# Second layer's projection weights: split into high and low parts ahead of time, or when they are used

## The chip, the cores and the metric

The kernel runs on one core of a Trainium2 chip. The metric is the time of one execution on the device, in microseconds (us), as the median of several runs. One execution was also taken with the hardware profiler; all rows below come from it.

## The reference

A stream of 512 latent tokens and a prefix of 256 context tokens, 1024 wide, pass through two layers. Cut to what matters here, a layer does:

```python
hl = modulate(rms_norm(x_lat, norm1_g), sh1, sc1)
p  = hl @ w_in            # columns: A (gMLP), Q, K, V, C (convolution), 512 each
pa, q, k, v, pc = split(p)                        # q, k: norm per head, rotary
ya = chunk_gmlp(pa)       # gelu, layer norm, 128x128 position mixing
o  = diff_attn(q, k_all, v_all)                   # keys: latent and context
yc = silu(layer_norm(dwconv31(glu(pc))))
x  = x + g1 * (concat(ya, rms_norm(o), yc) @ w_out)
h2 = modulate(rms_norm(x, norm2_g), sh2, sc2)
x  = x + g2 * ((silu(dwconv3(h2 @ w_gate)) * (h2 @ w_val)) @ w_down)
```

The first layer does this for latent and context tokens alike. In the second layer the context tokens only give keys and values. All numbers are float32, and the result has to be as close as float32 makes it.

## The kernel before

**Split products.** TensorE multiplies a reduced float32 form (float32r). To keep the precision, each operand is split into a high part, the value cast to float32r, and a low part, the value minus the high part, and a product is three matmuls: high by high, high by low, low by high. For activations this is done once. For a weight chunk it is done where the chunk is used: `wsplit` (L215) loads a raw chunk of 128x1024 on SP's queue (L212, tile `raw`, three buffers), casts it on ScalarE (L220, tile `whi`, two buffers) and subtracts on VectorE or GpSimd (`sub_lo`, L106, tile `wlo`, two buffers). The string `WE` says for each chunk of w_in which of the two engines subtracts (d or p), with one string for each layer.

**The order of the second layer.** A projection (`proj_tok`, L381) takes four chunks of w_in (128x1024 each, two blocks of the contraction), and for each chunk goes through its token tiles. The order is: K for the two context tiles, C (L432), A, K for the four latent tiles, Q, V for all six tiles; then attention in 16 units, with products of w_out as filler, then the rest of w_out and the feed-forward part. K's four chunks are thus split twice. Hooks at fixed steps of a projection put other work between its matmuls: the gate products `pg` of group A (L226 to L228 by the helper, from `vbh` of L496) and the transposes `pk` of K (L577, from `ks`).

**VectorE's work at that time.** The convolution of group C is 60 multiply-adds on VectorE (L647, tile `cacc`), at low priority. Beside them stand the statistics of A's layer norm (L482), its scaling (L494, L495), the norm and rotary of K and Q (L552 to L568, L591) and the low parts. GpSimd makes the rotary tables GC and GS (L543, L544), clears the convolution's input (L420) and has small copies and diagonals in attention.

**The feed-forward part** of the first layer runs in two halves of 11 blocks. In each half, 11 times, a gate and a value block are multiplied, convolved, gated and split into `gh` and `gl`; then four pairs of output blocks go through w_down in three chunks each. The rows of the adaLN modulation are computed on VectorE during the first half (`start_dots`, L918).

**What sets the order.** The program is written in plain order; a planner then orders the instructions of each engine by a priority that follows the program, by which `high_priority` moves instructions ahead and `low` back, and by its own estimate of when operands are ready. On the chip each engine and each queue keeps that order strictly: an instruction that waits holds up all behind it on its engine. Transfers issued on an engine's queue are instructions of that engine. All transfers of the kernel before are issued by SP. The kernel is built with `_BACC = {"dynamic_dma_scratch_size": 256}` (L1092), which the change leaves as it is.

Of the kernel before, what the change touches and what calls it, by code (L numbers as in the profile page):

```python
# [9 lines left out]
F32 = mybir.dt.float32  # L10
F32R = mybir.dt.float32r
# [40 lines left out]
DLOW, RLOW = 150, 250  # L52
CLOW = (4000, 1000)

WE = ("dpdpdpdddppdpppppddp", "pdpppppppppppppddpdd")

AH = ((4, 1), (18, 1))
KH = ((6, 10, 27, 31, 35, 39), (17, 17, 25, 34, 35, 48))
CH = ((41, 3), (40, 5))
N1H, N1P = 5, 2  # L60

VEV = 2

# [13 lines left out]
def tile_backbone(  # L77
# [137 lines left out]
    def wsplit(src, shape, eng="mix", raw=None, p=None, tags=("hi", "lo"), bufs=2):  # L215
# [6 lines left out]
            sub_lo(lo, raw, hi, e)  # L222
        return hi, lo

    def mm3(o, lhi, llo, rhi, rlo, start, stop):
        T.matmul(o, lhi, rhi, start=start, stop=False)  # L226
        T.matmul(o, lhi, rlo, start=False, stop=False)  # L227
        T.matmul(o, llo, rhi, start=False, stop=stop)  # L228
# [53 lines left out]
    for l in range(DEPTH):  # L282
# [26 lines left out]
        with ExitStack() as ph:  # L309
# [2 lines left out]
            ps = psum_pool(ph, f"ps1_{l}")  # L312

            def wengine(col, k2):
                return {"d": "dve", "p": "pool"}[WE[l][(col - COL_A) // 512 * 4 + k2]]

            def wsrc(col, k2):
                return w_in[l, 2 * k2 * P:(2 * k2 + 2) * P, col:col + 512].rearrange("(a p) n -> p a n", p=P)

            if l == 0:  # L320
                cs = sp.tile([P, KD, 32], F32, name="cs")
# [59 lines left out]
            def proj_tok(col, tiles, hooks=(), back=False):  # L381
                hooks, step = list(hooks), 0
                pt = {t: ps.tile([P, 512], F32, tag="acc", name="acc", bufs=6) for t in tiles}
                for k2 in range(KD // 2):
                    wh, wl = wsplit(wsrc(col, k2), [2, 512], wengine(col, k2))
                    for t in tiles:
                        for a in range(2):
                            hs = (slice(None), 2 * k2 + a, slice(t * P, (t + 1) * P))
                            T.matmul(pt[t], hhi[hs], wh[:, a], start=k2 + a == 0, stop=False)  # L389
                            T.matmul(pt[t], hlo[hs], wh[:, a], start=False, stop=False)  # L390
                        step += 1
                        for _, fn in [h for h in hooks if h[0] == step]:
                            fn()
                    for t in list(tiles)[::-1] if back and k2 == 3 else tiles:
                        for a in range(2):
                            hs = (slice(None), 2 * k2 + a, slice(t * P, (t + 1) * P))
                            T.matmul(pt[t], hhi[hs], wl[:, a], start=False, stop=k2 + 1 == KD // 2 and a == 1)  # L397
                        step += 1
                        for _, fn in [h for h in hooks if h[0] == step]:
                            fn()  # L400
                for _, fn in [h for h in hooks if h[0] > step]:
                    fn()
                return pt
# [26 lines left out]
                for o in px:  # L430
                    T.matmul(o.rearrange("p a n -> p (a n)"), z[:, :P], z, start=True, stop=False)
            for k2 in range(KD // 2):  # L432
                wh, wl = wsplit(wsrc(COL_C, k2), [2, 512], wengine(COL_C, k2), raw=pre.get(k2))
                for a in range(2):
                    k = 2 * k2 + a
                    for s in range(nseg)[::-1]:
                        t0, t1 = SEG[s]
                        for m in range(4):
                            ms = slice(m * P, (m + 1) * P)
                            o = pc[s][m][:, :t1 - t0]  # L440
                            T.matmul(o, wh[:, a, ms], hhi[:, k, t0:t1], start=k == 0 and s == 0, stop=False)
                            T.matmul(o, wh[:, a, ms], hlo[:, k, t0:t1], start=False, stop=False)
                            T.matmul(o, wl[:, a, ms], hhi[:, k, t0:t1], start=False,
                                     stop=k == KD - 1 and (s == 0 or m % 2 == 1))
# [50 lines left out]
            V.tensor_add(v, v, lnv[:, 1].unsqueeze(1).to_broadcast([P, NT, AW]))  # L495
            S.copy(vbh, v)  # L496
            sub_lo(vbl, v, vbh)
            wsh, wsl = wsplit(w_sT[l], [HEADS, P], p=sp, **(dict(bufs=1) if l else dict(tags=("mraw", "mraw"), bufs=MRB)))
            def a_finish():
                for h in range(HEADS):  # L500
                    yield
# [38 lines left out]
            nc.sync.dma_start(out=gbase, in_=qk_g[l])  # L540
            V.tensor_scalar_mul(gbase[:, 0], gbase[:, 0], QKD ** -0.5)
            for j in range(2):
                G.tensor_mul(GC[:, j], ropet[:, 0], gbase[:, j, 0].unsqueeze(1).to_broadcast([P, NLT, QKD]))  # L543
                G.tensor_mul(GS[:, j], ropet[:, 1], gbase[:, j, 1].unsqueeze(1).to_broadcast([P, NLT, QKD]))  # L544

            def qk_tile(x, t, j, r):

# [139 lines left out]
        yBl = yp.tile([P, 4, toks], F32R, name="yBl")  # L687

        def wout_w(mp2, parts, eng, **kw):
            return [(wsplit(w_out[l, q, mp2], [2, 4, P], eng, **kw), (yACh, yACl) if q == 0 else (yBh, yBl))  # L690
                    for q in parts]

        def wout(mp2, parts, w, segs, psf, tag, bufs, only=(0, 1)):
# [221 lines left out]
        with ExitStack() as ph:  # L915
# [22 lines left out]
            for half in range(2):  # L938
                gh = hp.tile([P, HJ, toks], F32R, tag="gh", name="gh", bufs=1)
                gl = hp.tile([P, HJ, toks], F32R, tag="gl", name="gl", bufs=1)  # L940
                for jj in range(HJ):
                    j = half * HJ + jj
                    pp = [[ps.tile([P, 512], F32, tag="acc", name="pp", bufs=8) for g in range(2)]
                          for s in range(nseg)]
                    w = [wsplit(w_gv[l, j, g], [KD, P], "dve") for g in range(2)]

                    def gv(g, seg):
                        a, b, s = seg
                        o = pp[s][g][:, a - SEG[s][0]:b - SEG[s][0]]
                        for k in range(KD):  # L950
                            mm3(o, w[g][0][:, k], w[g][1][:, k], hhi[:, k, a:b], hlo[:, k, a:b], k == 0, k == KD - 1)

                    if j == 0:
                        for seg in ngs:
                            if seg == g1:
                                for k in range(KD):
                                    r = norm2.apply(l, 1, g1, k, hhi, hlo)
                                tab["since"].append(r.ins)
                                table(T_SILU)
                            for g in range(2):  # L960
                                gv(g, seg)
                                if seg == g0 and g == 1:
                                    norm2.rstd(g1, ps, "acc", 8)
                    else:
                        for g in range(2):
                            for seg in whole:
                                gv(g, seg)
                    if j == 0 and not last:
                        start_dots(norm2.last)
                    t = sp.tile([P, TOK], F32, tag="ft", name="ft", bufs=FTB)  # L970
                    for s in range(nseg):
                        a, b = SEG[s]
                        gp = pp[s][0]
                        n = b - a
                        S.activation(t[:, a:b], gp[:, :n], AF.Identity, bias=fb[:, l, j:j + 1], scale=fw[:, l, j, 1:2])
                        V.scalar_tensor_tensor(out=t[:, a + 1:b], in0=gp[:, 0:n - 1], scalar=fw[:, l, j, 0:1],
                                               in1=t[:, a + 1:b], op0=ALU.mult, op1=ALU.add)
                        V.scalar_tensor_tensor(out=t[:, a:b - 1], in0=gp[:, 1:n], scalar=fw[:, l, j, 2:3],
                                               in1=t[:, a:b - 1], op0=ALU.mult, op1=ALU.add)
                    act(t[:, :toks], t[:, :toks], AF.Silu)  # L980
                    for s in range(nseg):
                        a, b = SEG[s]
                        V.tensor_mul(t[:, a:b], t[:, a:b], pp[s][1][:, :b - a])  # L983
                    S.copy(gh[:, jj], t[:, :toks])
                    sub_lo(gl[:, jj], t[:, :toks], gh[:, jj])
                chunks = [(j0, min(4, HJ - j0)) for j0 in range(0, HJ, 4)]
                for mp2 in range(KD // 2):
                    tail = half == 1 and mp2 == KD // 2 - 1
                    ws = {}
                    for gi, gs in enumerate([[g] for g in ngs] if tail else [whole]):  # L990
                        pd = {g: [ps.tile([P, 512], F32, tag="acc", name="pd", bufs=8) for i in range(2)] for g in gs}
                        cs_ = chunks[::-1] if gi else chunks
                        for ci, (j0, jn) in enumerate(cs_):
# [4 lines left out]
                            for jj in range(jn):  # L998
                                if gi and not last and (ci, jj) == (0, N1P):
                                    next_norm(ngs[0], ps, "acc", 8)  # L1000
                                st_, sp_ = ci == 0 and jj == 0, ci == len(cs_) - 1 and jj == jn - 1
                                for g in gs:
                                    a, b, s = g
                                    for i in range(2):
                                        ms = slice(i * P, (i + 1) * P)
                                        mm3(pd[g][i][:, :b - a], wh[:, jj, ms], wl[:, jj, ms],
                                            gh[:, j0 + jj, a:b], gl[:, j0 + jj, a:b], st_, sp_)
                        for g in gs:
                            a, b, s = g
                            for i in range(2):  # L1010
# [13 lines left out]
                if not last and half == 0:  # L1024
                    dots.close()
                    cstack.close()
                    wt = pool(ph, "wt", "left")
        pss_.close()
    hbs.close()
    nstack.close()  # L1030
# [84 lines left out]
```

## Time and profile before

| | |
|---|---|
| median of 3 runs | 1636.67 us (1635.95 to 1638.53) |
| the profiled execution | 1637.72 us, of which the span (first to last instruction) 1635.9 us |
| mean granted TensorE clock | 0.986 |
| TensorE (PE) busy | 1574.7 us, 96% |
| VectorE (DVE) busy | 1033.9 us, 63% |
| ScalarE (ACT) busy | 646.2 us, 40% |
| GpSimd (POOL) busy | 178.3 us, 11% |
| DMA | 162.08 MB, mean 99 GB/s |

Busy times of matmuls overlap at their ends, so a busy TensorE is not one at its peak. Rows of the trace name line, engine, operation and tiles as out<-in; a helper's line stands for all its callers, so the tile tells which call it is. A wait is put down to the instruction that released it. The second layer begins at about 968 us of the span, its attention at about 1143 us.

### The profile page before, as it was taken

The page shows a single profiled execution, that of the slowest core. Times are in us where ns is not written, and L with a number is a line of the kernel's source. Part 1 is how long each engine was busy: PE and PEld are TensorE (multiplying, and loading weights), DVE is VectorE, ACT ScalarE, POOL GpSimd, SP SyncE. Part 2 cuts the span into 40 slices and gives each one's busy share as a digit, 9 for nine tenths or more (in the row PEclk, how much of TensorE's full clock was granted, in tenths as well). Part 3 has the DMA queues.
Part 4 walks back from the last instruction along what each step waited for, and adds up shares of the span by engine and source line. Part 5 has one row for each costly group of instructions (what it writes and reads, how often), then busy time and mean ns, then how long its engine had stood idle before and what let it go on. Part 6 is the DMA issues. An engine that isn't in the chain of part 4 may idle for free.

```text
span 1635.9 us, 20796 instructions
## 1 busy us (share of the span) xinstructions
PE 1574.7 (96%) x8186; PEld 1294.7 (79%) x8186; DVE 1033.9 (63%) x1666; ACT 646.2 (40%) x1098; POOL 178.3 (11%) x158
## 2 busy tenths in 40 slices
PE   7999998999999999999999999779999999999999
PEld 5865776778888888888888878567778788888888
DVE  4597878969999862244333277996987544244433
ACT  5431568753523221133232244255775433123321
POOL 1130224310000000000000023341420000000000
PEclk8999999999999999999999999889999999999999
DMA  8625110014355852111122223221001223332232
GB/s 286 201 96 171 42 62 14 14 64 169 104 193 194 290 192 70 66 65 62 56 65 58 84 87 110 62 65 52 27 27 65 91 90 96 88 101 97 96 100 94
DMA packets 57409, 162.08 MB, mean 99 GB/s; under 512 B 9056, under 2 KB 11360, under 8 KB 57184
## 3 DMA queue, kind: packets, MB, share of 16 engines
q1 hardware_dynamic: 57312, 160.76, 30.3%
q8 instruction: 64, 1.05, 0.3%
q14 instruction: 33, 0.27, 0.0%
HBM read 158.64 MB, written 2.10 MB: 98 GB/s over the span
## 4 chain that ended last, share of the span: by engine, by line
PE 83%; DVE 10%; ACT 4%; issue 1%; DMA 1%; POOL 0%; POOLq 0%; DVEq 0%; SPq 0%; ACTq 0%
PE pp L227 13%; PE pp L226 13%; PE pp L228 13%; PE pd L228 6%; PE pd L226 6%; PE pd L227 6%; PE acc L389 4%; PE acc L390 4%; PE acc L397 3%; DVE cacc L647 3%; PE po L816 2%; PE mr L156 2%; PE wo L226 1%; PE wo L227 1%; PE wo L228 1%
## 5 line engine op out<-in xcount | busy, mean ns | idle before, releaser
L220 ACT CAST whi<-raw 128x1024 fp32r<-128x1024 f32 (+2 forms) x199 | 204.3, 1029 | 550.9 <-PE pp L227 251.0
L106 DVE TENSOR_TENSOR wlo<-raw,whi 128x1024 fp32r<-128x1024 f32 (+1 forms) x163 | 196.9, 1210 | 304.9 <-ACT whi L220 297.4
L227 PE MATMUL pp<-hlo,whi 128*128 128x512 f32 (+1 forms) x1072 | 380.7, 356 | 0.8 <-DVE hlo L266 0.8
L226 PE MATMUL pp<-hhi,whi 128*128 128x512 f32 (+1 forms) x1072 | 379.8, 356 | 1.5 <-ACT whi L220 1.3
L228 PE MATMUL pp<-hhi,wlo 128*128 128x512 f32 (+1 forms) x1072 | 378.9, 354 | 0.0
L226 PEld LDWEIGHTS pp<-hhi,whi 128*128 128x128 f32 x1072 | 201.4, 188 | 35.1 <-ACT whi L220 2.7
L227 PEld LDWEIGHTS pp<-hlo,whi 128*128 128x128 f32 x1072 | 201.5, 188 | 33.0 <-DVE hlo L266 1.5
L228 PEld LDWEIGHTS pp<-hhi,wlo 128*128 128x128 f32 x1072 | 201.5, 188 | 31.0
L106 POOL TENSOR_TENSOR wlo<-raw,whi 128x1024 fp32r<-128x1024 f32 (+1 forms) x36 | 100.3, 2788 | 870.3 <-ACT whi L220 716.9
L228 PE MATMUL pd<-gh,wlo 128*128 128x512 f32 (+1 forms) x550 | 192.4, 350 | 0.6 <-DVE wlo L106 0.6
L226 PE MATMUL pd<-gh,whi 128*128 128x512 f32 (+1 forms) x550 | 192.9, 351 | 0.0
L227 PE MATMUL pd<-gl,whi 128*128 128x512 f32 (+1 forms) x550 | 192.3, 350 | 0.0
L389 PE MATMUL acc<-whi,hhi 128*128 128x512 f32 x352 | 144.8, 411 | 2.8 <-ACT whi L220 2.8
L390 PE MATMUL acc<-whi,hlo 128*128 128x512 f32 x352 | 144.2, 410 | 0.0
L647 DVE SCALAR_TENSOR_TENSOR cacc<-cin,cw,cacc 128x783 f32<-128x783 f32 (+1 forms) x120 | 125.8, 1102 | 2.8 <-ACT cacc L642 2.7
L228 PEld LDWEIGHTS pd<-gh,wlo 128*128 128x128 f32 x550 | 103.4, 188 | 15.9 <-DVE wlo L106 0.8
L227 PEld LDWEIGHTS pd<-gl,whi 128*128 128x128 f32 x550 | 103.5, 188 | 15.1
L226 PEld LDWEIGHTS pd<-gh,whi 128*128 128x128 f32 x550 | 103.4, 188 | 14.9
L983 DVE TENSOR_TENSOR ft<-ft,pp 128x256 f32<-128x256 f32 (+1 forms) x66 | 39.4, 598 | 96.2 <-PE pp L228 84.7
L397 PE MATMUL acc<-wlo,hhi 128*128 128x512 f32 x352 | 94.0, 401 | 0.0
L389 PEld LDWEIGHTS acc<-whi,hhi 128*128 128x128 f32 x352 | 68.0, 193 | 25.0 <-issue 7.1
L192 DVE CUSTOM_DVE_ANT_0 mraw<-mraw,csil,bmod 128x1024 f32<-128x1024 f32 x64 | 81.7, 1280 | 8.0 <-DMA mraw<-in_w_modT_dram 7.8
(198 smaller groups left out, 2334.3 us busy)
## 6 DMA issues: line engine op xcount, KB each, us to landing
raw<-in_w_gv_dram SPq DMA_DIRECT2D x88, 512.0 KB, 3.2
mraw<-in_w_modT_dram SPq DMA_DIRECT2D x64, 512.0 KB, 4.2
raw<-in_w_in_dram SPq DMA_DIRECT2D x44, 512.0 KB, 3.6
raw<-in_w_down_dram SPq DMA_DIRECT2D x34, 512.0 KB, 3.6
mraw<-in_w_modN_dram SPq DMA_DIRECT2D x16, 512.0 KB, 5.9
mraw<-in_w_modH_dram SPq DMA_DIRECT2D x16, 512.0 KB, 3.9
raw<-in_w_out_dram SPq DMA_DIRECT2D x16, 512.0 KB, 3.2
raw<-in_w_down_dram SPq DMA_DIRECT2D x16, 384.0 KB, 3.2
```

The lines of the kernel that those rows point to most:

```text
L106: (eng or V).tensor_sub(o, a, hi.bitcast(F32))
L156: T.matmul(o[r:r + 32], cs[:, k], w, start=k < 4, stop=k >= 4, tile_position=(0, r))
L192: r = V.tensor_tensor_reduce(out=junk, in0=w, in1=csil[:, s], scale=1.0, scalar=bmod[:, l, i, f:f + 1], op0=ALU.mult, op1=ALU.add, accum_o ...
L220: S.copy(hi, raw)
L226: T.matmul(o, lhi, rhi, start=start, stop=False)
L227: T.matmul(o, lhi, rlo, start=False, stop=False)
L228: T.matmul(o, llo, rhi, start=False, stop=stop)
L389: T.matmul(pt[t], hhi[hs], wh[:, a], start=k2 + a == 0, stop=False)
L390: T.matmul(pt[t], hlo[hs], wh[:, a], start=False, stop=False)
L397: T.matmul(pt[t], hhi[hs], wl[:, a], start=False, stop=k2 + 1 == KD // 2 and a == 1)
L647: V.scalar_tensor_tensor(out=cacc[:, c, :cn], in0=cin[:, c, j:j + cn], scalar=cw[:, l, c, j:j + 1], in1=cacc[:, c, :cn], op0=ALU.mult, op1 ...
L983: V.tensor_mul(t[:, a:b], t[:, a:b], pp[s][1][:, :b - a])
```

## The change

High and low parts of the second layer's w_in (20 chunks) and w_out (8 chunks) are made during the second half of the first layer's feed-forward part and stored in device memory. `split_ahead` is a generator of 56 units: each loads half a chunk (128x512), casts it on ScalarE, subtracts on VectorE and stores both parts; all three transfers are issued by GpSimd. After each of the 11 gate and value blocks three units are drawn (`AHEAD[0]`), after each chunk of w_down eight (`AHEAD[1]`), until none is left, with a priority 60 places later. In the second layer `wsplit_of` loads the two ready parts of a chunk, again on GpSimd's queue; in w_in every second chunk uses two of the three `raw` buffers for its parts. GC and GS, in both layers, move from GpSimd to VectorE, and the low part of w_s is always made on VectorE. The second string of `WE` goes.

```diff
+AHEAD = (3, 8)
+ALOW = 60
+    dram = ctx.enter_context(tc.tile_pool(name="split", bufs=1, space=bass.MemoryType.DRAM))
+    split = {}
+    def split_ahead(sp):
+        todo = [(("in", col, k2), [w_cols(1, col, k2)[:, a] for a in range(2)])
+                for col in (COL_K, COL_C, COL_A, COL_Q, COL_V) for k2 in range(KD // 2)]
+        todo += [(("out", q, mp2), [w_out[1, q, mp2, :, i].rearrange("p k m -> p (k m)") for i in range(2)])
+                 for mp2 in range(KD // 2) for q in range(2)]
+        for key, srcs in todo:
+            split[key] = dram.tile([P, 2, 2, 512], F32, name="_".join(map(str, key)))
+            for a, src in enumerate(srcs):
+                raw = sp.tile([P, 512], F32, tag="araw", name="araw", bufs=3)
+                hi = sp.tile([P, 512], F32R, tag="ahi", name="ahi", bufs=3)
+                G.dma_start(out=raw, in_=src)
+                S.copy(hi, raw)
+                sub_lo(raw, raw, hi)
+                G.dma_start(out=split[key][:, 0, a], in_=hi.bitcast(F32))
+                G.dma_start(out=split[key][:, 1, a], in_=raw)
+                yield
+    def wsplit_of(key, src, shape, eng, tags=("hi", "lo"), p=None, **kw):
+        if key not in split:
+            return wsplit(src, shape, eng, p=p, **kw)
+        r = []
+        for x, t in enumerate(tags):
+            w = (p or wp).tile([P] + shape, F32R, tag=t, name="w" + "hl"[x], bufs=RAWB if t == "raw" else 2)
+            flat = w.rearrange("p a n -> p a n") if len(shape) == 2 else w.rearrange("p a k m -> p a (k m)")
+            G.dma_start(out=flat, in_=split[key][:, x])
+            r.append(w)
+        return r
...
+            def wchunk(col, k2, **kw):
+                tags = ("raw", "raw") if k2 % 2 else ("hi", "lo")
+                return wsplit_of(("in", col, k2), wsrc(col, k2), [2, 512], wengine(col, k2), tags, **kw)
...
-                    wh, wl = wsplit(wsrc(col, k2), [2, 512], wengine(col, k2))
+                    wh, wl = wchunk(col, k2)
...
-            wsh, wsl = wsplit(w_sT[l], [HEADS, P], p=sp, **(...))
+            wsh, wsl = wsplit(w_sT[l], [HEADS, P], "dve", p=sp, **(...))
...
-                G.tensor_mul(GC[:, j], ropet[:, 0], gbase[:, j, 0].unsqueeze(1).to_broadcast([P, NLT, QKD]))
+                V.tensor_mul(GC[:, j], ropet[:, 0], gbase[:, j, 0].unsqueeze(1).to_broadcast([P, NLT, QKD]))
...
+                    if not last and half:
+                        with low(ALOW):
+                            for _ in zip(range(AHEAD[0]), ahead):
+                                pass
...
+                    ahead = split_ahead(wt)
```

## Rows read from the trace of the kernel before

**Rows 1.** The profile's page: busy us with share of the span, and GB/s in 40 slices.

```profile
PE 1574.7 (96%) x8186; PEld 1294.7 (79%) x8186; DVE 1033.9 (63%) x1666; ACT 646.2 (40%) x1098; POOL 178.3 (11%) x158
...
GB/s 286 201 96 171 42 62 14 14 64 169 104 193 194 290 192 70 66 65 62 56 65 58 84 87 110 62 65 52 27 27 65 91 90 96 88 101 97 96 100 94
```

**Rows 2.** Waits of TensorE in 940 to 1260 us: waiting group, releaser, us, times, longest.

```profile
PE pk L577 <- DVE ks L106: 10.9, 3, 4.5
PE pg L226 <- ACT vbh L496: 8.7, 1, 8.7
PE acc L389 <- ACT whi L220: 2.8, 1, 2.8
```

**Rows 3.** Stretches: window and length, busy us (instructions) by engine, PEclk, DMA share, GB/s.

```profile
706.00:875.00 169.00, 169.00 (x962) 147.19 (x961) 68.15 (x91) 51.36 (x63) 0.00 (x0) 1.00 0.19 62
1003.70:1026.10 22.40, 22.40 (x98) 17.99 (x97) 21.23 (x20) 9.53 (x14) 9.93 (x4) 1.00 0.37 111
1026.10:1114.00 87.90, 64.77 (x286) 50.61 (x285) 84.71 (x135) 37.67 (x72) 28.98 (x13) 0.86 0.20 62
1051.00:1056.00 5.00, 4.18 (x13) 3.42 (x14) 4.15 (x8) 0.02 (x1) 0.00 (x0) 0.55 0.01 3
1087.00:1094.00 7.00, 6.69 (x23) 5.56 (x24) 6.25 (x19) 4.02 (x9) 0.00 (x0) 0.57 0.28 77
```

**Rows 4.** VectorE in order of time: start us, us, line, form [idle before].

```profile
1007.38 28.34 DVE L647 SCALAR_TENSOR_TENSOR cacc<-cin,cw,cacc 128x512 f32<-128x512 f32 x28 [0.80 <-ACT cacc L642]
1035.64 0.75 DVE L482 BATCH_NORM_STATS2 st<-v 128x6 f32<-128x256 f32 x2
...
1049.81 1.41 DVE L647 SCALAR_TENSOR_TENSOR cacc<-cin,cw,cacc 128x512 f32<-128x512 f32 x2
...
1076.15 2.37 DVE L557 TENSOR_TENSOR nw<-nw,rk 128x8 f32<-128x8 f32 x1
...
1082.61 0.16 DVE L557 TENSOR_TENSOR nw<-nw,rk 128x8 f32<-128x8 f32 x1
...
1084.03 2.54 DVE L567 TENSOR_TENSOR kx<-kx,GC 128x512 f32<-128x512 f32 x1
...
1095.22 2.88 DVE L591 TENSOR_TENSOR kx<-kx,rk 128x512 f32<-128x512 f32 x1
```

**Rows 5.** GpSimd (POOL) in order of time, same columns.

```profile
1009.59 4.55 POOL L106 TENSOR_TENSOR wlo<-raw,whi 128x1024 fp32r<-128x1024 f32 x2 [8.02 <-ACT whi L220]
...
1075.13 3.37 POOL L106 TENSOR_TENSOR wlo<-raw,whi 128x1024 fp32r<-128x1024 f32 x1 [4.66 <-ACT whi L220]
```

**Rows 6.** Groups by form in 790 to 1230 us: busy us, mean ns.

```profile
L647 DVE SCALAR_TENSOR_TENSOR cacc<-cin,cw,cacc 128x512 f32<-128x512 f32 x60 | 62.6, 1095 | 0.8 <-ACT cacc L642 0.8
...
L106 DVE TENSOR_TENSOR ks<-kx,ks 128x512 fp32r<-128x512 f32 x6 | 4.1, 681 | 1.4 <-ACT ks L595 1.4
...
L565 DVE TENSOR_TENSOR qsq<-kx,GS 128x256 f32<-128x256 f32 x8 | 3.3, 416 | 0.0
```

**Rows 7.** ScalarE groups by form in 790 to 1230 us.

```profile
L220 ACT CAST whi<-raw 128x512 fp32r<-128x512 f32 x1 | 0.6, 621 | 0.0
```

**Rows 8.** DMA issues in 790 to 1230 us: count, KB each, us from issue to landing.

```profile
raw<-in_w_in_dram SPq DMA_DIRECT2D x24, 512.0 KB, 3.6
...
lnv<-in_lnv_gb_dram SPq DMA_DIRECT2D x1, 256.0 KB, 2.6
```

**Rows 9.** TensorE in order of time, start of layer 2 and its first long wait.

```profile
968.08 0.40 PE L389 MATMUL acc<-whi,hhi 128*128 128x512 f32 x1
...
1040.21 0.50 PE L389 MATMUL acc<-whi,hhi 128*128 128x512 f32 x1 [2.75 <-ACT whi L220]
...
1051.07 0.58 PE L226 MATMUL pg<-vbh,whi 128*128 128x256 f32 x1 [8.74 <-ACT vbh L496]
```

**Rows 10.** ScalarE in order of time: first and last of 11 casts of the second half.

```profile
706.04 0.84 ACT L984 CAST gh<-ft 128x768 fp32r<-128x768 f32 x1
...
874.84 0.83 ACT L984 CAST gh<-ft 128x768 fp32r<-128x768 f32 x1
```

More of the change, by code (lines that the diff above doesn't have):

```diff
@@ L53 @@
 CLOW = (4000, 1000)
-WE = ("dpdpdpdddppdpppppddp", "pdpppppppppppppddpdd")
+WE = "dpdpdpdddppdpppppddp"
+AHEAD = (3, 8)
 AH = ((4, 1), (18, 1))
@@ L223, in wsplit, with w_cols @@
         return hi, lo
+    dram = ctx.enter_context(tc.tile_pool(name="split", bufs=1, space=bass.MemoryType.DRAM))
+    split = {}
+    def w_cols(l, col, k2):
+        return w_in[l, 2 * k2 * P:(2 * k2 + 2) * P, col:col + 512].rearrange("(a p) n -> p a n", p=P)
+    def split_ahead(sp):
[24 more added lines that the diff above has]
+        return r
     def mm3(o, lhi, llo, rhi, rlo, start, stop):
@@ L314, in wengine @@
             def wengine(col, k2):
-                return {"d": "dve", "p": "pool"}[WE[l][(col - COL_A) // 512 * 4 + k2]]
+                return {"d": "dve", "p": "pool"}[WE[(col - COL_A) // 512 * 4 + k2]]
             def wsrc(col, k2):
-                return w_in[l, 2 * k2 * P:(2 * k2 + 2) * P, col:col + 512].rearrange("(a p) n -> p a n", p=P)
+                return w_cols(l, col, k2)
+            def wchunk(col, k2, **kw):
+                tags = ("raw", "raw") if k2 % 2 else ("hi", "lo")
+                return wsplit_of(("in", col, k2), wsrc(col, k2), [2, 512], wengine(col, k2), tags, **kw)
             if l == 0:
@@ L432, in tile_backbone @@
             for k2 in range(KD // 2):
-                wh, wl = wsplit(wsrc(COL_C, k2), [2, 512], wengine(COL_C, k2), raw=pre.get(k2))
+                wh, wl = wchunk(COL_C, k2, raw=pre.get(k2))
                 for a in range(2):
@@ L497, in tile_backbone @@
             sub_lo(vbl, v, vbh)
-            wsh, wsl = wsplit(w_sT[l], [HEADS, P], p=sp, **(dict(bufs=1) if l else dict(tags=("mraw", "mraw"), bufs=MRB)))
+            wsh, wsl = wsplit(w_sT[l], [HEADS, P], "dve", p=sp, **(dict(bufs=1) if l else dict(tags=("mraw", "mraw"), bufs=MRB)))
             def a_finish():
@@ L542, in tile_backbone @@
             for j in range(2):
-                G.tensor_mul(GC[:, j], ropet[:, 0], gbase[:, j, 0].unsqueeze(1).to_broadcast([P, NLT, QKD]))
-                G.tensor_mul(GS[:, j], ropet[:, 1], gbase[:, j, 1].unsqueeze(1).to_broadcast([P, NLT, QKD]))
+                V.tensor_mul(GC[:, j], ropet[:, 0], gbase[:, j, 0].unsqueeze(1).to_broadcast([P, NLT, QKD]))
+                V.tensor_mul(GS[:, j], ropet[:, 1], gbase[:, j, 1].unsqueeze(1).to_broadcast([P, NLT, QKD]))
             def qk_tile(x, t, j, r):
@@ L689, in wout_w @@
         def wout_w(mp2, parts, eng, **kw):
-            return [(wsplit(w_out[l, q, mp2], [2, 4, P], eng, **kw), (yACh, yACl) if q == 0 else (yBh, yBl))
+            return [(wsplit_of(("out", q, mp2), w_out[l, q, mp2], [2, 4, P], eng, **kw), (yACh, yACl) if q == 0 else (yBh, yBl))
                     for q in parts]
@@ L1007, in tile_backbone @@
                                             gh[:, j0 + jj, a:b], gl[:, j0 + jj, a:b], st_, sp_)
+                        if not last and half:
+                            with low(ALOW):
+                                for _ in zip(range(AHEAD[1]), ahead):
+                                    pass
                         for g in gs:
```

## Prediction

> **What bounds the kernel now.** I read the page first: TensorE is busy 96% of the span, and in most slices it does not wait at all [rows 1]. So a change to VectorE, ScalarE or GpSimd work can only pay where TensorE waits. The waits of TensorE name that place for the second layer [rows 2]: the gate product pg waits 8.7 us for the cast of vbh, three transposes of K wait 10.9 us for ks, and one product waits 2.8 us for a cast weight. All of it lies in one stretch: from 1026.1 to 1114 TensorE is busy 64.8 of 87.9 us, so 23.1 us are lost, while VectorE is busy 84.7 of 87.9 [rows 3]. In the neighbouring stretch 1003.7 to 1026.1 TensorE is full. [...]
>
> Why VectorE is late is seen when its order of time is laid beside GpSimd's. Two multiply-adds of the convolution follow each other in 1.41 us, 0.70 each [rows 4], yet the 60 of them take 62.6 us, 1095 ns on average [rows 6]. A square of eight numbers takes 2.37 us at 1076.15 and 0.16 at 1082.61; at 1075.13 GpSimd had begun a subtraction that made a weight's low part, and the long one ends as that one does [rows 4, 5]. The 28 multiply-adds that take 28.34 us from 1007.38 (28 x 0.70 would be 19.6) hold two such subtractions from 1009.59 on, and more after them. So GpSimd's subtractions hold VectorE up. The sum of what they cost between 1003.7 and 1114: 62.6 - 60 x 0.70 = 20.6 on the convolution, 2.37 - 0.16 = 2.2, 2.54 - 0.68 = 1.9 and 2.88 - 0.68 = 2.2 on three others [rows 4, 6], together 26.9 us.
>
> [...]
>
> **The change part by part.** (1) Removed in layer 2: 24 splits of w_in (K is split twice) and 8 of w_out, each a load on SP, a cast on ScalarE and a subtraction on GpSimd or VectorE. With the subtractions goes the 26.9 us of hold-up. What is late next: VectorE's own work. Between 1003.7 and 1114 it is busy 21.2 + 84.7 = 105.9 us [rows 3]; less 26.9 it is 79.0; plus what moves to it (below, 2.4) 81.4. [...] As a check, the first wait: the statistics start at 1035.64 behind 28 multiply-adds [rows 4], which without GpSimd end at 1007.4 + 19.6 = 1027; that is 8.6 us earlier, and pg waited 8.7 [rows 9], with one cast's 2.75 before it gone as well. I therefore take three quarters of 23.1 + 4.8 = 27.9: a gain of 21 us. Its bounds: 28 if nothing is left over, 0 if VectorE's order keeps it late all the same.
>
> (2) Moved: GC and GS go from GpSimd to VectorE, 4 products at 0.42 [rows 6], 1.7 us in each layer, and the low part of w_s, at most 0.7. Counted above for layer 2. In layer 1 the products sat on GpSimd, where by the same mechanism they cost VectorE as much; I take 0, and 2 us at most if it meets a wait.
>
> (3) Added in layer 1, second half of the feed-forward part: 56 units, each a 256 KB load, a 128x512 cast, a 128x512 subtraction and two 256 KB stores. ScalarE: 56 x 0.62 = 35 us [rows 7], VectorE: 56 x 0.68 = 38 us [rows 6]. From 706 to 875 ScalarE is busy 51 and VectorE 68 of 169 us, GpSimd 0, and TensorE 169 [rows 3]; there the next weights are cast well ahead, so the work fits beside the matmuls: 1 us. What can break the cover is the queue: 3 x 56 = 168 transfers go through GpSimd's queue in order, and ScalarE, which also works in order, stands at a cast whose load is late, with the casts of the feed-forward weights and with them TensorE behind it. The units start with the first gh of that half, at 706 [rows 10], and layer 2 starts at 968.08 [rows 9]: 262 us, 1.56 us for each transfer. The trace has no transfer on that queue. Bounds from the rows: the highest rate of a slice is 290 GB/s [rows 1], 0.90 us for 256 KB; one at a time on SP's queue takes 2.6 us from issue to landing [rows 8]. SP's 512 KB loads take 3.6 us each [rows 8] and the slice's rate is two of them in the air, so I take the lower end for the forecast and keep the other as a rival.
>
> (4) Added in layer 2: 32 x 2 loads of 512 KB on GpSimd's queue in place of 32 on SP's. A step of four tiles is 22.4 / 4 = 5.6 us of TensorE [rows 3] and needs two of them: 2 x 1.8 at 290 GB/s is covered, 2 x 3.6 one behind the other is not. Behind a load that waits for its buffer stand, in GpSimd's order, the clearing of cin and the copies and diagonals of attention; before, they stood behind subtractions that waited for the same buffers. 1 us.
>
> Sum, against the profiled execution (1637.72 us, of which 1635.9 are span): 1637.7 - 21 + 1 + 1 = 1618.7. The median of the runs is 1.05 us under that execution, so I say 1618.
>
> **Rivals.** First, VectorE stays the bound: the convolution's 60 multiply-adds still need 42 us between A's projection and the end of Q, and TensorE's order was planned elsewhere. [...] Against: the first wait vanishes in the check above. Half the gain is left, 1637.7 - 14 + 2 = 1626.
>
> Second, layer 2's loads are late: two at 3.6 us are 7.2 against a step of 5.6, 1.6 us on each of the 16 steps of C, A, K and Q, 25.6 us; what fits in the buffers ahead of time takes back about 7. 1637.7 - 19 + 18.6 = 1637, no change.
>
> Third, the other side: the transfers of the preparation go one at a time. The place is GpSimd's queue between 706 and 968; it decides from 1.56 us per transfer on. At 2.6 us, 168 take 437 us and end at 1143, so layer 2 starts 175 us late; its 48 loads of w_in at 3.6 then take 173 us, to 1316, and the last step of V (six tiles, 8.4 us) ends at 1324 where it ended at 1143.5: 1637.7 + 181 = 1818. At 2.0 us the preparation ends at 1042, 74 us late, with the gain kept 1693. For it: no row shows two transfers of that queue in the air, and the kernel gives it 256 bytes of scratch. Against: SP's queue overlaps its own.
>
> [...]
>
> **How the numbers follow.** Forecast 43%, first rival 12%, second 8%, third 37%. About 0.2%, 3.3 us, is what a measurement of this kernel can tell from no change. Faster: forecast and first rival, nearly, 0.54; same: most of the second, 0.07; slower: the third and the rest of the second, 0.39. The likeliest case's own range is 1607 (a gain of 28 and some waits of attention) to 1630. The whole range has to reach into the third rival up to its one-at-a-time price: 1607 to 1820; above it lies a spacing that is longer than SP's 2.6 us, below it a gain that this stretch does not hold.
>
> **What would show it.** Right: no GpSimd subtraction between 1003 and 1144, convolution steps at 0.70 to 0.75 us all along, pg and pk without waits over 2 us, TensorE still full from 706 to 968. First rival: pk still waiting for ks. Second: TensorE waiting for DMA in A, K and Q at each step. Third: ScalarE waiting for the raw pieces of the preparation, TensorE idle in the second half of layer 1's feed-forward part, and layer 2's first matmul after 1030. My forecast is wrong if TensorE's busy share falls below 95%.

## The result, and the profile after

| | before | after |
|---|---|---|
| median | 1637.32 us (4 runs beside the ones of after) | 2038.23 us (4 runs) |
| span of the profiled execution | 1635.9 us | 2037.0 us |
| mean granted TensorE clock | 0.986 | 0.900 |
| TensorE busy | 96% | 80% |

The change is a loss: 1.2449 times the time before, interval [1.2428, 1.2471]. The prediction of 1618 us was wrong, with its range; what came is the third rival, and worse than it was priced.

One thing in the description of the kernel has to be put right: the eight units of `AHEAD[1]` are drawn after each pair of output blocks, not after each chunk of w_down. And the planner did not keep to those places, for a lower priority is no date: ScalarE's first cast of the preparation stands at 599.06, behind the last cast of gh of the first half (596.37), while the program draws the first units behind the first gh of the second half, here at 961.09. So the transfers begin at 596, at the end of the first half.

TensorE's slices of the kernel before, which [rows 1] leaves out:

```profile
PE   7999998999999999999999999779999999999999
...
PEclk8999999999999999999999999889999999999999
```

The page after, busy times ([rows 1] has those of before) and the same slices:

```profile
PE 1638.2 (80%) x8186; PEld 1338.8 (66%) x8186; DVE 1021.5 (50%) x1722; ACT 647.9 (32%) x1122; POOL 231.8 (11%) x358
...
PE   7999999999992444325344899977799889999999
...
PEclk8999999999996666667677899988899989999999
```

Slices 13 to 22 (a slice is 51 us) hold most of the loss: TensorE is busy between two and five tenths there, and its granted clock falls to six and seven tenths. The same as stretches (columns as in [rows 3]): the preparation, the rest of layer 1, and layer 2 from its first matmul to the end of V:

```profile
620.00:1141.00 521.00, 208.43 (x882) 173.96 (x883) 86.93 (x123) 64.59 (x93) 87.77 (x161) 0.67 0.30 101
1141.00:1308.00 167.00, 167.00 (x951) 145.71 (x950) 60.61 (x80) 44.82 (x56) 1.09 (x2) 1.00 0.22 69
1334.90:1529.00 194.10, 158.79 (x649) 123.88 (x649) 107.93 (x219) 57.08 (x109) 24.97 (x45) 0.90 0.42 128
```

As soon as the last store is issued, at 1138.51, TensorE is full again. Its longest waits, over the whole span (waiting group, releaser, us, times, longest):

```profile
PE pp L266 <- ACT whi L224: 154.2, 12, 20.8
PE pd L266 <- ACT whi L224: 153.9, 9, 22.0
PE acc L441 <- DMA wl<-in: 24.0, 7, 6.0
PE accC L487 <- DMA wl<-in: 11.3, 2, 7.5
PE wo L266 <- DMA wh<-out: 8.2, 2, 4.6
```

The waits of [rows 2] are gone. In their place TensorE waits 308 us for casts of feed-forward weights. ScalarE in order of time shows why:

```profile
657.71 0.62 ACT L248 CAST ahi<-araw 128x512 fp32r<-128x512 f32 x1 [21.18 <-DMA araw<-in_w_in_dram]
661.02 0.62 ACT L248 CAST ahi<-araw 128x512 fp32r<-128x512 f32 x1 [2.69 <-DMA araw<-in_w_in_dram]
664.23 0.62 ACT L248 CAST ahi<-araw 128x512 fp32r<-128x512 f32 x1 [2.59 <-DMA araw<-in_w_in_dram]
664.75 1.04 ACT L224 CAST whi<-raw 128x1024 fp32r<-128x1024 f32 x1
685.91 0.62 ACT L248 CAST ahi<-araw 128x512 fp32r<-128x512 f32 x1 [20.11 <-DMA araw<-in_w_in_dram]
```

Three casts of the preparation stand between two casts of feed-forward weights, so each such weight has to wait until three units have gone through GpSimd's queue. GpSimd over the same time:

```profile
654.79 0.54 POOL L247 DMA_DIRECT2D araw<-in_w_in_dram  x1 [2.46 <-issue]
657.95 0.55 POOL L247 DMA_DIRECT2D araw<-in_w_in_dram  x1 [2.62 <-issue]
661.26 0.54 POOL L247 DMA_DIRECT2D araw<-in_w_in_dram  x1 [2.76 <-issue]
664.43 0.55 POOL L250 DMA_DIRECT2D in<-ahi  x1 [2.64 <-issue]
...
682.98 0.55 POOL L247 DMA_DIRECT2D araw<-in_w_in_dram  x1 [2.44 <-issue]
```

An issue shows 0.55 us, and then the queue stands for some 2.5 us with "issue" as the reason, that is, for nothing that the profile shows. Nine transfers, 654.79 to 682.98, take 28.2 us; ScalarE's cycle from one group to the next, 657.71 to 685.91, is the same 28.2. A transfer lands after 2.6 to 2.9 us, as on SP's queue [rows 8], and the next one starts some 0.3 us after that: one at a time.

The convolution of layer 2, the group of [rows 6], now without GpSimd's subtractions (busy us, mean ns):

```profile
L691 DVE SCALAR_TENSOR_TENSOR cacc<-cin,cw,cacc 128x512 f32<-128x512 f32 x60 | 41.5, 744 | 1.4 <-ACT cacc L686 1.4
```

So the part that the forecast was about did happen: 1095 ns became 744. Layer 2 nevertheless takes 34.3 us longer, 2037.0 - 1334.9 = 702.1 against 1635.9 - 968.1 = 667.8, because its own loads come 4.3 us apart (below). With 1334.9 - 968.1 = 366.8 us for the late start that makes 401.1, the difference of the two spans.

### The profile page after: what moved, and what is told of

It reads as the page before. It is cut to its first block, busy times and chain, and to the rows that moved or that the text cites. A ratio compares the mean times of both kernels' runs of the same rounds, so it can differ in the third digit from the quotient of the medians.

```text
span 2037.0 us, 21259 instructions
## 1 busy us (share of the span) xinstructions
PE 1638.2 (80%) x8186; PEld 1338.8 (66%) x8186; DVE 1021.5 (50%) x1722; ACT 647.9 (32%) x1122; POOL 231.8 (11%) x358
## 4 chain that ended last, share of the span: by engine, by line
PE 56%; issue 25%; DMA 5%; DVE 5%; POOL 4%; ACT 3%; POOLq 0%; DVEq 0%; ACTq 0%; SPq 0%
PE pp L267 8%; PE pp L266 8%; PE pp L268 8%; PE pd L268 4%; PE pd L267 4%; PE pd L266 4%; PE acc L441 3%; PE acc L433 3%; PE acc L434 3%; PE po L860 2%; DMA araw<-in_w_in_dram 2%; DMA mraw<-in_w_modT_dram 2%; PE wo L268 1%; PE wo L266 1%; PE wo L267 1%
## 5 line engine op out<-in xcount | busy, mean ns | idle before, releaser
L266 PE MATMUL pp<-hhi,whi 128*128 128x512 f32 (+1 forms) x1072 | 392.2, 367 | 154.4 <-ACT whi L224 154.2
L268 PE MATMUL pp<-hhi,wlo 128*128 128x512 f32 (+1 forms) x1072 | 390.2, 365 | 5.0 <-DVE wlo L110 5.0
L110 DVE TENSOR_TENSOR wlo<-raw,whi 128x1024 fp32r<-128x1024 f32 (+2 forms) x154 | 185.3, 1205 | 230.3 <-ACT whi L224 223.3
L224 ACT CAST whi<-raw 128x1024 fp32r<-128x1024 f32 (+1 forms) x167 | 170.8, 1024 | 399.0 <-PE pp L267 211.3
L110 DVE TENSOR_TENSOR araw<-araw,ahi 128x512 f32<-128x512 f32 x56 | 38.7, 692 | 439.2 <-ACT ahi L248 439.2
L248 ACT CAST ahi<-araw 128x512 fp32r<-128x512 f32 x56 | 34.6, 617 | 468.7 <-DMA araw<-in_w_in_dram 343.6
L691 DVE SCALAR_TENSOR_TENSOR cacc<-cin,cw,cacc 128x783 f32<-128x783 f32 (+1 forms) x120 | 103.4, 914 | 3.4 <-ACT cacc L686 3.4
L433 PE MATMUL acc<-whi,hhi 128*128 128x512 f32 x192 | 77.8, 405 | 0.0
L434 PE MATMUL acc<-whi,hlo 128*128 128x512 f32 x192 | 77.0, 401 | 0.0
L101 ACT ACTIVATE e<-pss,mx 128x768 f32<-128x768 f32 (+1 forms) x80 | 65.2, 818 | 14.7 <-DVE mx L815 14.0
```

Of the source, the lines that this page charges most:

```text
L101: r = S.activation(out, in_, func, **kw)
L110: (eng or V).tensor_sub(o, a, hi.bitcast(F32))
L224: S.copy(hi, raw)
L691: V.scalar_tensor_tensor(out=cacc[:, c, :cn], in0=cin[:, c, j:j + cn], scalar=cw[:, l, c, j:j + 1], in1=cacc[:, c, :cn], op0=ALU.mult, op1 ...
```

## The experiments

All numbers are to be read beside 1637 us for the kernel before, which ran beside each group of them on the same chip (medians 1637.25 to 1638.21). Where an interval or several executions are named, a kernel ran four or five times; the others ran once. Executions of one kernel lay up to 4.6 us apart, but for one that is named below. Three questions: why does GpSimd's queue stand, what would the change be worth without that, and is the gain in layer 2 what the prediction said it was. Where a scratch size isn't named it is 256 bytes, as in before and after.

**The room of GpSimd's queue, alone.** One number:

```diff
-_BACC = {"dynamic_dma_scratch_size": 256}
+_BACC = {"dynamic_dma_scratch_size": 1024}
```

> The changed kernel with 1024 bytes of scratch in place of 256; the order of all engines is the same. Theory A (256 bytes hold one transfer of GpSimd's queue, so each waits until the one before has landed): several are in the air, the issues of the preparation follow each other at 0.6 to 1.6 us and not 2.9 to 3.3, ScalarE no longer waits 20 us at a time for araw, layer 2 begins before 1000 us and not at 1335; time 1610 to 1645. Theory B (an issue on GpSimd costs about 3 us by itself, whatever the room): spacing and time stay, 2038. Theory C (the DMA engines are the limit): the same, 2038.

Measured: 1656.94 us (ratio to before 1.0112 [1.0095, 1.0129]), with the order of every engine unchanged from after. One number took 381 of the 401 us back, so the room is the cause (A); an issue does not cost 3 us by itself (B: those at 602.35, 602.88 and 603.41 follow each other after 0.53), and the DMA engines carry the load (C): in the preparation's stretch they move 250 GB/s. The preparation, and layer 2 from K to the end of V:

```profile
597.00:811.00 214.00, 182.97 (x937) 153.38 (x935) 84.29 (x124) 62.67 (x92) 91.01 (x168) 0.93 0.77 250
...
1015.80:1160.30 144.50, 144.50 (x653) 115.27 (x652) 107.74 (x220) 56.98 (x110) 25.37 (x46) 1.00 0.58 179
```

The part from K to V in the kernel before:

```profile
968.10:1143.40 175.30, 151.47 (x653) 119.13 (x652) 148.12 (x219) 80.29 (x134) 55.17 (x24) 0.93 0.25 75
```

With TensorE full and at full clock it takes 144.5 us instead of 175.3. The 30.8 us are 23.8 of idle time and 7.0 of matmul time that the lower clock had cost (151.5 against 144.5). After V layer 2 is 2.8 us longer than before (495.3 against 492.5); TensorE waits there for the first ready parts of w_out:

```profile
PE wo L266 <- DMA wh<-out: 3.8, 2, 2.2
```

That leaves 28.0 us for layer 2 as a whole. The time was still 12 us above what was expected, because layer 2 starts at 1015.8, 47.7 us late; 47.7 - 28.0 = 19.7 is what makes this kernel slower than before (spans of 1655.6 and 1635.9).

With room for 320 bytes:

> The changed kernel with 320 bytes of scratch. Theory A: 320 bytes hold two transfers and not three, the preparation goes at about half the spacing, near 1.5 to 1.7 us, 168 of them need 250 to 285 us where 262 were at hand; time 1620 to 1720. Theories B and C: 2038.

Measured: 1747.74 us, slower than expected; 168 issues from 597.16 to 896.85, 1.79 us apart on average, and layer 2 at 1100.4. How many transfers are in flight is seen where GpSimd's queue had been idle for some time: in order 256 bytes (after), 320, and 512 bytes (a kernel that comes below):

```profile
595.93 0.76 POOL L247 DMA_DIRECT2D araw<-in_w_in_dram  x1 [248.70 <-DVE amod L205]
599.35 0.56 POOL L247 DMA_DIRECT2D araw<-in_w_in_dram  x1 [2.67 <-issue]
```

```profile
597.16 1.31 POOL L247 DMA_DIRECT2D araw<-in_w_in_dram  x2 [248.72 <-DVE amod L205]
600.66 0.55 POOL L247 DMA_DIRECT2D araw<-in_w_in_dram  x1 [2.19 <-issue]
```

```profile
705.99 1.14 POOL L253 DMA_DIRECT2D in<-ahi  x2 [25.98 <-ACT ahi L250]
707.40 0.54 POOL L254 DMA_DIRECT2D in<-araw  x1 [0.27 <-issue]
710.68 0.55 POOL L254 DMA_DIRECT2D in<-araw  x1 [2.75 <-issue]
```

One, then a wait; two, then a wait; three, then a wait. With 1024 bytes six follow each other without one (shown with the kernel e11_paced_three, below).

**The two halves of the change, each alone**, at 256 bytes. First the preparation, with layer 2 splitting its weights as before:

```diff
-        if key not in split:
+        if True:
```

> Only the first half of the change, with 256 bytes: the parts are made and stored, but layer 2 loads and splits its weights as before and never reads them. If the preparation alone makes the layer-1 loss (layer 2 begins 367 us later), time 1637 + 367 = 2004. Rival: the late start is made by layer 2's loads queueing on GpSimd behind the stores; then the time is near 1640.

Measured: 2002.73 us. Then the use, with two units prepared and all loads of layer 2 reading that one pair:

```diff
-        for key, srcs in todo:
-            split[key] = dram.tile(...)
+        for key, srcs in todo[:1]:
+            one = dram.tile(...)
+            for k, _ in todo:
+                split[k] = one
```

> Only the second half of the change, with 256 bytes: two units are prepared and every load of layer 2 reads that one pair of parts (the numbers are therefore not those of the reference). Theory A: layer 1 as before, layer 2 from its first projection to the end 702 us as in the changed kernel against 668 before, so 1637 + 34 = 1671, TensorE waiting for wl in C, A, K and Q. Rival (the loads are hidden and layer 2's loss is the late weights' doing): 1610 to 1640.

Measured: 1671.74 us. The halves, 365 and 34, make nearly the whole 401. So at this size even the use alone loses, though GpSimd's subtractions are gone: TensorE waits 26.0 + 10.4 us for `wl` in the projections and 8.1 for `wh` of w_out, and the loads of 512 KB go one at a time:

```profile
971.40 0.53 POOL L263 DMA_DIRECT2D wl<-one  x1 [3.75 <-PE acc L443]
975.90 0.53 POOL L263 DMA_DIRECT2D wl<-one  x1 [3.96 <-issue]
980.35 0.53 POOL L263 DMA_DIRECT2D wh<-one  x1 [3.92 <-issue]
```

The use alone with 1024 bytes:

> Scratch 1024 bytes; two units are prepared and all of layer 2's ready-made loads read that one pair, so the preparation is all but left out (the numbers computed are not the reference's). Theory (what the change removes in layer 2 is worth 28 us once the loads of its queue overlap): 1605 to 1614. Rival (part of layer 2's shorter time came from something else, such as the late start giving it an emptier queue or a later clock): 1620 or more.

Measured: 1607.67 us, 30 below before. This is what the change is worth when its preparation costs next to nothing.

**Is the order of ScalarE what is left at 1024 bytes?** The units are drawn three at each gh and two at each chunk of w_down, and each unit's cast is ordered behind the ScalarE cast at its own place in the program:

```diff
-                S.copy(hi, raw)
+                r = S.copy(hi, raw)
+                tc.add_manual_dep(r.ins, here[0].name, NOSYNC, reason="paced")
```

(`here[0]` is the last cast of a feed-forward weight or of gh; the edge only fixes ScalarE's order, without a semaphore.)

> Scratch 1024 bytes, the preparation's units drawn three at each gh and two at each chunk of w_down, and each unit's cast tied behind the ScalarE cast at its own place in the program, so that ScalarE never has three preparation casts between two consecutive w_down weights. Theory (the 47.7 us that were left with 1024 bytes come from ScalarE's order, not from the transfers): layer 2's first matmul at 965 to 980, as before (968.1), TensorE's waits for whi gone from the second half of the feed-forward part, layer 2 as short as with 1024 bytes (28 us less than before); in all 1605 to 1622. Rival (three buffers of raw pieces and 5 us for a load set the pace whatever the order): layer 2 starts at 1000 to 1020 and the time is 1645 to 1660.

Measured: 1628.29 us, 0.9942 [0.9925, 0.9959] of before. Better than before, but above the 1605 to 1622 expected: layer 2 started at 989.6. The stretch of the gh blocks, 706 to 875, is full (169.0 of 169), so what was left lies in w_down alone, where 23 units were left, and six of their casts still stood ahead of the last cast of a w_down weight:

```profile
PE pd L268 <- ACT whi L225: 15.9, 4, 11.6
```

The same order with 256 bytes:

> The paced order with the scratch left at 256 bytes. Theory (256 bytes hold one transfer of GpSimd's queue, 2.9 us each, whatever the order): 168 transfers need about 490 us from 706 on, so layer 2 starts at 1190 or later and its loads at 4.3 us are late too; 1850 to 2000. Rival (the order alone was the cause): under 1680.

Measured: 1983.77 us, layer 2 at 1270.0. The order alone cures little; both conditions are needed.

**Is it GpSimd's subtractions that hold VectorE up?** The paced kernel, with 24 subtractions put back on GpSimd that nothing needs:

```diff
+                if l and k2 % 2:
+                    idle = wp.tile([P, 2, 512], F32, tag="raw", name="idle", bufs=RAWB)
+                    same = ident.unsqueeze(1).to_broadcast([P, 8, P])
+                    for _ in range(2):
+                        G.tensor_sub(idle.rearrange("p a (b n) -> p (a b) n", n=P), same, same)
```

> The paced kernel, with GpSimd subtractions put back in layer 2 that nothing needs: two of 128x1024 at each odd chunk of w_in, reading a constant tile, 24 in all; the weights are still loaded ready made, so neither a cast nor a subtraction of a weight is on the way to TensorE. Theory (GpSimd subtractions hold VectorE up, which is what the change took away): the convolution's 60 multiply-adds go from 0.75 back to about 1.0 us on average, TensorE waits for ks and for vbh come back, 8 to 27 us more than the paced kernel. Rival (the gain came from work that VectorE, ScalarE or SP no longer has, and GpSimd's own work is harmless): within 3 us of the paced kernel.

Measured: 1656.09 us, 27.8 above the paced kernel and so just over the 27 expected (1.0107 [1.0092, 1.0122] and 0.9942 [0.9925, 0.9959] of before). The convolution's mean went from 748 to 959 ns, and TensorE's waits of [rows 2] are back, the one of pg with 8.4 us where it was 8.7 before, those of pk with 5.9 where they were 10.9:

```profile
PE pg L268 <- ACT vbh L548: 8.4, 1, 8.4
PE pk L629 <- ACT kk L631: 3.2, 1, 3.2
PE pk L629 <- DVE ks L110: 2.7, 1, 2.7
```

```profile
L699 DVE SCALAR_TENSOR_TENSOR cacc<-cin,cw,cacc 128x512 f32<-128x512 f32 x60 | 54.6, 959 | 1.4 <-ACT cacc L694 1.4
```

In order of time, VectorE and then GpSimd:

```profile
1050.32 7.33 DVE L699 SCALAR_TENSOR_TENSOR cacc<-cin,cw,cacc 128x512 f32<-128x512 f32 x6
...
1061.26 6.05 DVE L699 SCALAR_TENSOR_TENSOR cacc<-cin,cw,cacc 128x512 f32<-128x512 f32 x4
```

```profile
1052.15 4.30 POOL L369 TENSOR_TENSOR idle<-ident 128x1024 f32<-128x1024 f32 x2
...
1061.24 4.19 POOL L369 TENSOR_TENSOR idle<-ident 128x1024 f32<-128x1024 f32 x2 [1.02 <-PE acc L449]
```

Six multiply-adds at 0.70 are 4.2 us and took 7.33; four are 2.8 and took 6.05. The excess is 3.1 and 3.3 us, and each time two subtractions lie in that time. The weights came ready made in both kernels, so the casts and subtractions that VectorE, ScalarE and SP no longer do are not the cause. From K to the end of V this kernel takes 171.8 us and the paced one 145.2: the 26.6 between them are the whole of the difference, which is 27.8 by the medians and 23.4 between the two profiled executions. GpSimd's subtractions take 53.7 us in this part; before it was 49.1 for low parts and 4.8 for GC and GS, so as much was put back as the change had taken away. The subtractions also push back GpSimd's loads; TensorE's waits for those are 2.7 us in this part, a small share.

**Can the preparation be hidden?** Four units for each of the eleven steps, one at each chunk of w_down:

> As the paced kernel (scratch 1024 bytes), with the units drawn earlier: one behind each w_gate and w_up weight's cast and two behind each gh, four for each of the eleven steps, and one at each chunk of w_down, so that no preparation is left beside the last w_down weights. Theory (what the paced kernel lost, 20 us against 1608, lies in its 15.9 us of waits for whi in w_down, where 23 units were left over): layer 2 starts at 966 to 980, no wait for whi over 2 us, 1605 to 1615, and the kernel beats the one before by 1.4 to 2%. Rival (the preparation costs about 20 us wherever it is put, by the transfers it lays beside those of the weights): 1622 to 1632.

Measured: 1622.89 us, 0.9912 [0.9899, 0.9926]: by its time inside the rival's range, layer 2 at 980.7. In place of 18.4 us of waits for whi and wlo, one of them 11.6, there were thirteen short ones, 11.1 us in all, 8.3 of them in the steps that three units for each step had left full. The same kernel again, under a label that names another size (its scratch has 1024 bytes):

> The kernel e9_paced_two once more on this chip, for one look beside it: within 4 us of it.

Measured: 1626.34 us. So the start was moved forward as well: 12 units each behind a w_down cast of the first half, three or four behind each gh, and six at the first chunks of w_down:

```diff
+                            if not last and not half:
+                                early.append(here[0])
...
+                    with low(ALOW):
+                        for _ in zip(early[:], ahead):
+                            pass
```

> Scratch 1024 bytes; the first 12 units are each tied behind a w_down cast of the first half, where GpSimd's queue is empty, then three or four behind each gh, and the last six at the first chunks of w_down; nothing is left beside the last w_down weights. Theory (the 15 us by which e9_paced_two is above the 1608 of the kernel that hardly prepares anything are its many waits for whi and wlo of 0.5 to 2 us, because four units for each step are more than the three buffers of raw pieces carry): layer 2 starts at 964 to 972, 1606 to 1615. Rival (the preparation costs 15 us by its transfers beside the weights' wherever it is put): 1620 to 1630.

Measured: 1606.6 us, 0.9808 [0.9788, 0.9827]. One of its four executions took 5401.5 us. The same kernel again:

> The kernel e11_paced_three once more, in more rounds: one of its four timed executions had taken 5401.5 us. If that one was a disturbance from outside the kernel, all executions lie between 1604 and 1612; if the kernel's own queues can get stuck (GpSimd's loads of layer 2 behind stores, for instance), executions of several thousand us come back.

Measured: 1607.4 us, 0.9814 [0.98, 0.9827], all five executions between 1606.45 and 1608.25; the long one did not come back, and what it was stays open. The kernel beats both before and after, the one before by the 30 us that the use alone was worth; so the rival, that the preparation costs 15 us wherever it is put, falls. TensorE is full through the whole preparation, and the issues follow each other (rows of e11_paced_three):

```profile
580.00:706.00 126.00, 126.00 (x718) 109.71 (x718) 55.42 (x79) 29.66 (x39) 21.54 (x40) 1.00 0.53 170
706.00:875.00 169.00, 169.00 (x957) 146.92 (x956) 88.37 (x127) 68.95 (x96) 57.05 (x106) 1.00 0.67 224
875.00:968.00 93.00, 93.00 (x525) 80.69 (x524) 40.92 (x68) 26.80 (x44) 18.09 (x33) 1.00 0.50 161
```

```profile
705.75 1.14 POOL L253 DMA_DIRECT2D in<-ahi  x2 [26.12 <-ACT ahi L250]
707.17 1.15 POOL L254 DMA_DIRECT2D in<-araw  x2 [0.28 <-issue]
708.37 0.54 POOL L253 DMA_DIRECT2D in<-ahi  x1
708.97 0.54 POOL L254 DMA_DIRECT2D in<-araw  x1
```

The same kernel with 512 bytes, and with 256 bytes and the preparation's transfers on SP's queue:

> The kernel e11_paced_three with a scratch of 512 bytes. With 256 bytes transfers of GpSimd's queue follow each other after 2.9 us, with 320 after about 1.8. Theory (the room sets how many overlap, and the paced order needs about 1.7 us per transfer over the time it has): 512 bytes are nearly enough, 1606 to 1640. Rival (only a room for very many transfers helps): 1700 or more.

Measured: 1614.54 us. Three in flight are nearly enough.

> The order of e11_paced_three, scratch back at 256 bytes, and the preparation's loads and stores on SP's queue; layer 2's ready-made loads stay on GpSimd's. Theory (the room of 256 bytes binds GpSimd's queue alone; the same transfers on SP's overlap): layer 2 starts at 965 to 985, and only its own loads at 4.3 us are late, as in the use-only kernel with 256 bytes: 1655 to 1690. Rival (the 168 transfers are slow by themselves, whatever the queue, by their pieces of 4 KB or by DRAM): 1750 or more.

Measured: 1668.35 us, layer 2 at 964.5, TensorE full up to there. On SP's queue the same 168 transfers are hidden at 256 bytes; the 31 us above before are layer 2's own loads, still on GpSimd's queue and 4.3 us apart.

## Why the prediction was wrong

**The step that failed is (3), "Added in layer 1": the price of a transfer on GpSimd's queue.** It had two ends, 0.90 us and 2.6 us, and took the lower one for the forecast because SP's queue overlaps its loads (290 GB/s in a slice [rows 1], as much as two loads of 512 KB in 3.6 us [rows 8]). Measured: 542.6 us from the first issue to the last, 3.25 us from one of the 168 to the next (in the cycle of nine above, 3.13). The nearest row was no row of that queue, and the line that decided was in the code and not in the trace: the scratch of 256 bytes, which no row of the kernel before shows at work, as SP issued everything there. The prediction named it as what spoke for the third rival and still gave that rival only 37%.

**The third rival was the case, and its price of 1818 was 220 us short.** Its mechanism and its signs were right: ScalarE waits for raw pieces, TensorE stands in layer 1's feed-forward part, its busy share is far under 95%. Its place was right only in part: half of the 308 us, the waits of pd, lie in w_down of the first half, before the second half's first matmul at 889.8. Three sizes were wrong. A transfer took 3.25 us, not 2.6. The preparation began at 596, not at 706, because the planner put it ahead of its place in the program; so it ended at 1141, almost where the rival had it (1143), by two errors that cancel. And the decisive one: the rival let layer 2 start when the preparation ended, as if layer 1 went on beside it. But ScalarE holds the feed-forward weights behind the preparation's casts, so layer 1 itself went at the preparation's pace: 208 us of matmul time, at a mean clock of 0.67, in 521. When the preparation ended, 194 us of layer 1 and its norm were still to come. So the stall of ScalarE, which both streams share in order, was not paid beside the work but added to it.

**Part (1), the gain in layer 2, was right, and its size too careful.** Forecast 21 with 28 as its bound; measured from K to V 30.8 with e1_room_1024 and 30.1 with the paced kernel, and e8_hold shows that GpSimd's subtractions are the cause of nearly all of it: 26.6, of which 2.7 are waits for the loads that they push back. Nothing was left over. No run shows the 4.8 us that the prediction's sum adds to its 23.1; the lower clock, 0.93 against 1.00, had cost 7.0 us of matmul time from K to V (151.5 against 144.5). The convolution went to 744 to 748 ns, as said (0.70 to 0.75), and pk and pg wait no more. VectorE's own work, 81.4 us by the prediction, was no obstacle: TensorE is full from K to V in e1_room_1024 (144.5 of 144.5 us), so the first rival was not the case.

GpSimd's issues of transfers did VectorE no harm: in after, 18 multiply-adds of the convolution follow each other in 12.07 us from 1394.74 on, 0.67 each, with issues at 1398.17 and 1402.44 among them. Two subtractions cost VectorE 3.1 to 3.3 us (e8_hold).

**Part (4), layer 2's loads, was taken at 1 us.** At 256 bytes it is 34 us against before, and as layer 2 should have gained 28, some 62; at 1024 bytes TensorE waits 0.3 us at most for its loads from K to V (e1_room_1024, e5_paced, e14_paced_three_again) and 3.6 to 4.4 us after V for the first parts of w_out. The second rival had the mechanism (two loads for each step, one behind the other) and a price of 25.6 at 3.6 us for a load; the load came at 4.3.

**Part (2), the products moved to VectorE, was taken at 0 in layer 1, 2 us at most; the runs show 3 there.** From the first gate product pg to the first matmul on tile cm, with the transposes of K between them, TensorE has the same 251 matmuls and takes 52.8 us before and 49.8 or 49.9 in each of the kernels with the change. The start of cm, before and in the kernel that only prepares (pg stands at 152.20 and 152.35):

```profile
204.97 1.02 PE L609 MATMUL cm<-cin,ones 128*128 128x512 f32 x2
```

```profile
202.17 1.02 PE L653 MATMUL cm<-cin,ones 128*128 128x512 f32 x2
```

Up to there the change alters nothing in layer 1 but GC, GS and the low part of w_s; which of them it is was not tried. In layer 2 the kernel that only prepares, with its splits as before, takes 173.6 us from K to V instead of 175.3, in one execution. So of the 30 us that the last kernel gains, 3 are layer 1's: its layer 2 starts at 965.0 instead of 968.1.

**The room of a transfer is known by counts alone.** On GpSimd's queue one, two, three and six transfers of 256 KB were issued without a wait at 256, 320, 512 and 1024 bytes (after, e2_room_320, e12_paced_three_512, e11_paced_three). That a transfer waits for room in the scratch is what these counts suggest; what it puts there, and how many bytes, no run shows. The same 168 transfers on SP's queue at 256 bytes held nothing up: layer 2 starts at 964.5 (e13_prepare_on_SP_256).

## What to carry to other kernels

Before transfers are moved to a queue that the profile has not shown, find what bounds how many it holds in flight (here the scratch: one at 256 bytes, three at 512), and price them one at a time until a run shows otherwise. Work that is put beside a full engine has to be placed against the order of every engine that it shares: here a lower priority did not pace it (its first cast came at 599 us, not behind the gh at 961.09), and a late load ahead of a cast stopped all that was behind it, TensorE for up to 22.0 us at a time. And a change that loses 400 us can hold a gain of 30: its halves, run alone, told in two runs which one to mend.

## What the runs showed of the hardware

That GpSimd's queue stood is not seen in its busy time: in after it shows 0.54 us for an issue and 11% busy for the span, while its queue set the pace for 540 us; only the idle time "<-issue", some 2.5 us before most rows, tells it. The hold between GpSimd and VectorE went both ways in e8_hold: two subtractions that take 3.9 to 4.4 us at four other places (3.88 at 1025.08, 4.30 at 1052.15, 4.19 at 1061.24, 4.39 at 1086.69) show 10.84 us where VectorE ran 21 multiply-adds in a row (GpSimd's spans are rough, but the excess is over 6 us):

```profile
1027.16 15.61 DVE L699 SCALAR_TENSOR_TENSOR cacc<-cin,cw,cacc 128x512 f32<-128x512 f32 x21 [1.44 <-ACT cacc L694]
```

```profile
1035.65 10.84 POOL L369 TENSOR_TENSOR idle<-ident 128x1024 f32<-128x1024 f32 x2 [1.02 <-PE acc L449]
```
